# One load instead of two for the first buffer, and fifteen short reads from GpSimd, in a row-sum kernel

## The chip, the cores and the metric

The kernel runs on one core of a Trainium2 chip. The metric is device time in microseconds, the median of seven runs: 162.25 us for the kernel before (162.16 to 162.47). A core has several engines that run side by side and wait for each other through semaphores. Here VectorE (DVE) and ScalarE (ACT) add, SyncE (SP) issues the loads, and GpSimd (POOL) does next to nothing. The transfers themselves run on 16 DMA engines, which are fed by queues: one queue for the DMAs that SP issues, one for those of ScalarE.

## The reference

```python
def setup_inputs():
    batch, seq, dim = 32, 512, 1024
    return {
        "x": np.random.randn(batch, seq, dim).astype(np.float32),
    }

def reference(x: np.ndarray) -> np.ndarray:
    return np.sum(x, axis=-1).astype(np.float32)
```

The input has 16,384 rows of 1024 float32 numbers, 67.1 MB in all. The output is the sum of each row.

## The kernel before

The 16,384 rows are dealt out to 128 partitions, 128 rows each, in two blocks (`BLOCKS = (112, 16)`). In a block, each partition holds consecutive rows of x: 112 in the first block, 16 in the second. The rows are loaded into buffers `xt` of 16 rows per partition (`G = 16`, 64 KB per partition, 8 MB in all), of which there are three in turn. The first block is seven such buffers; the second is one.

For each of the first six buffers one VectorE instruction (line 43, `tensor_reduce`, in `rows_dve`) sums all 16 rows and writes 16 columns of the block's result tile `res`. Of the seventh buffer VectorE sums nine rows and ScalarE seven (line 51, one row per instruction). Then ScalarE sends the first block's result to memory (line 89).

The last buffer is loaded in five smaller pieces (lines 95 and 98: 9, 4 and 2 rows, then the last row in two parts), so that less is left to sum when the last bytes land. VectorE and ScalarE share its rows; the last ones are added in pairs of halves (line 59) with a small copy between (line 112). SP sends the last result (line 114).

What sets the order around the change:

- The first buffer is loaded in two parts. Line 78 makes the parts: row 0 of each partition, then rows 1 to 15. Both are issued at line 81, as all whole buffers are. The reduce of this buffer reads all 16 rows and waits for both parts.
- Loads of the second and third buffer need no wait. The load of the fourth waits until the first reduce is over, since it overwrites the first buffer, and so on.
- After the program is built, `tile_reduce_tiled_1024_kernel` takes the first `EARLY = 2` DMA instructions of SP out of the main part and puts them into the opening part, ahead of a barrier that all engines pass. These are the two loads of the first buffer.
- At the end SP waits for the semaphores of all DMAs, in pairs, and then all engines pass the closing barrier (line 120).

Of the kernel before, what the change touches and what calls it, by code (L numbers as in the profile page):

```python
# [1 line left out]

# [4 lines left out]

F32 = mybir.dt.float32
ADD = mybir.AluOpType.add
COPY = mybir.ActivationFunctionType.Copy  # L10
X = mybir.AxisListType.X

BLOCKS = (112, 16)
G = 16
ACT_ROWS = 7
CUT = 544
EARLY = 2


@with_exitstack  # L20
def row_sums(
    ctx: ExitStack,
    tc: tile.TileContext,
    x: bass.AP,
    out: bass.AP,
):
    nc = tc.nc
    P = nc.NUM_PARTITIONS

    x_flat = x.flatten_outer_dims()  # L30
    R, D = x_flat.shape
    C = R // P
    assert R % P == 0 and sum(BLOCKS) == C
    out_flat = out.rearrange("a (b c) -> (a b c)", c=1)

    xpool = ctx.enter_context(tc.tile_pool(name="x", bufs=3))
    rpool = ctx.enter_context(tc.tile_pool(name="res", bufs=1))
    part = rpool.tile([P, 1], F32, name="part")
    seen = rpool.tile([P, 1], F32, name="seen")
    pairs = [rpool.tile([P, D // 2], F32, name=f"pairs{i}") for i in range(3)]  # L40

    def rows_dve(xt, res, j, n, c):
        nc.vector.tensor_reduce(  # L43
            out=res[:, c : c + n],
            in_=xt[:, j * D : (j + n) * D].rearrange("p (j d) -> p j d", d=D),
            axis=X,
            op=ADD,
        )

    def sum_act(v, acc):  # L50
        nc.scalar.activation(out=v, in_=v, func=COPY, accum_out=acc)  # L51

    def rows_act(xt, res, j, n, c):
        for i in range(n):
            sum_act(xt[:, (j + i) * D : (j + i + 1) * D], res[:, c + i : c + i + 1])

    def pairs_dve(xt, a, b, first, acc, pairs):
        h = (a + b) // 2
        nc.vector.tensor_tensor_reduce(  # L59
            out=pairs[:, 0 : h - a], in0=xt[:, a:h], in1=xt[:, h:b], scale=1.0, scalar=first,  # L60
            op0=ADD, op1=ADD, accum_out=acc,
        )

    def block(r0, n):
        x_b = x_flat[r0 : r0 + P * n].rearrange("(p c) d -> p (c d)", p=P)
        out_b = out_flat[r0 : r0 + P * n].rearrange("(p c) -> p c", p=P)
        return x_b, out_b, rpool.tile([P, n], F32, name=f"res{r0}")

    full = C - G
    done = 0  # L70
    for b, n in enumerate(BLOCKS):
        x_b, out_b, res = block(done * P, n)
        final = b == len(BLOCKS) - 1
        whole = n - G if final else n
        c = 0
        while c < whole:
            m = min(G, whole - c)
            xt = xpool.tile([P, G * D], F32, tag="xt", name="xt")
            parts = (0, 1, m) if done + c == 0 else (0, m)
            for i, k in zip(parts, parts[1:]):  # L80
                nc.sync.dma_start(
                    out=xt[:, i * D : k * D], in_=x_b[:, (c + i) * D : (c + k) * D]
                )
            a = ACT_ROWS if done + c + m == full else 0
            rows_dve(xt, res, 0, m - a, c)
            rows_act(xt, res, m - a, a, c + m - a)
            c += m
        if not final:
            nc.scalar.dma_start(out=out_b, in_=res)
        done += n  # L90

    xt = xpool.tile([P, G * D], F32, tag="xt", name="xt")
    cuts = [0, 9, 13, 15]
    for i, k in zip(cuts, cuts[1:]):
        nc.sync.dma_start(out=xt[:, i * D : k * D], in_=x_b[:, (c + i) * D : (c + k) * D])  # L95
    last = 15 * D
    for i, k in ((0, CUT), (CUT, D)):
        nc.sync.dma_start(
            out=xt[:, last + i : last + k],
            in_=x_b[:, c * D + last + i : c * D + last + k],  # L100
        )

    for i, k in zip(cuts[:2], cuts[1:3]):
        h = (k - i) // 2
        rows_dve(xt, res, i, h, c + i)
        rows_act(xt, res, i + h, k - i - h, c + i + h)
    pairs_dve(xt, 13 * D, 14 * D, 0.0, res[:, c + 13 : c + 14], pairs[2])
    rows_act(xt, res, 14, 1, c + 14)
    pairs_dve(xt, last, last + CUT, 0.0, part, pairs[0])


    nc.vector.tensor_copy(out=seen, in_=part)  # L112
    pairs_dve(xt, last + CUT, last + D, part, res[:, c + 15 : c + 16], pairs[1])
    nc.sync.dma_start(out=out_b, in_=res)


def kernel(tc: tile.TileContext, x: bass.AP, out: bass.AP):
    row_sums(tc, x, out)
    tc.close()
    tc.compile()  # L120

    sp = mybir.EngineType.SP
    fn = tc.nc.m.functions[0]
    entry, body = None, None
    for blk in fn.blocks:
        ops = [i for i in blk.instructions if i.engine == sp]
        if entry is None:
            entry = blk  # L130
        elif any(i.opcode == "DMACopy" for i in ops):
            body = blk
            break
    code = list(body.instructions)
    loads = [i for i in code if i.engine == sp][:EARLY]
    for load in loads:
        assert load.opcode == "DMACopy" and not load.sync_info.on_wait
        code.remove(load)
    body.instructions = code
    code = list(entry.instructions)  # L140
    at = next(k for k, i in enumerate(code) if i.engine == sp and i.opcode == "Drain")
    code[at:at] = loads
    entry.instructions = code

# [1 line left out]
_INS = ['x']  # L146
_OUTS = [((32, 512), 'float32')]


# [23 lines left out]
```

## Time and profile before

| | |
|---|---|
| median of 7 runs | 162.25 us (162.16 to 162.47) |
| the profiled execution | 162.38 us, of which the span from first to last instruction is 160.6 us |
| VectorE busy | 121.5 us, 76% of the span |
| ScalarE busy | 17.2 us, 11% |
| GpSimd busy | 0.2 us (four small fills at the start) |
| read from memory | 67.11 MB, a mean of 418 GB/s over the span |

The profile follows one execution. It says how long each engine was busy, what ended each of its idle times, and which chain of work ended last. It also gives the DMA queues with the number and size of their packets: `q1` is the queue of SP, `q10` that of ScalarE. For each group of DMA issues it gives the time from issue to landing, which includes the time that a DMA stands behind others in its queue. "L43" is line 43 of the kernel; "x6" means six instructions.

### The profile page before, as it was taken

To read this page: it belongs to the slowest core of one execution; us is meant where nothing else is said; L and a number is where in the kernel's file an instruction comes from. 1 tells how busy PE (TensorE), PEld (TensorE's weight loads), DVE (VectorE), ACT (ScalarE), POOL (GpSimd) and SP (SyncE) were. 2 spreads that over 40 slices of the span, in tenths; PEclk is the share of its full clock that TensorE was granted. 3 is DMA by queue.
4 is the path that set the end of the run, shared out by engine and by line. 5 is a ranking of instruction groups with operands and counts; after the bars stand their busy time and mean duration, and the time that the engine had idled before them with its cause. 6 is when DMAs were issued, how large, how long until landed. Compare 5 with 4: busy or idle time off the path is not lost.

```text
span 160.6 us, 119 instructions
## 1 busy us (share of the span) xinstructions
DVE 121.5 (76%) x16; ACT 17.2 (11%) x31; POOL 0.2 (0%) x4
## 2 busy tenths in 40 slices
DVE  0000059997799958999499994999949998698874
ACT  0000000000000000000000000000000000595892
POOL 0000000000000000000000000000000000000000
DMA  9988996996996996996996996996996997998990
GB/s 375 490 367 367 490 522 261 522 522 261 522 522 261 522 506 278 522 506 278 522 506 278 522 506 278 522 506 278 522 490 294 522 473 310 441 441 367 444 384 28
DMA packets 2160, 67.18 MB, mean 418 GB/s; under 512 B 496, under 2 KB 624, under 8 KB 880
## 3 DMA queue, kind: packets, MB, share of 16 engines
q1 hardware_dynamic: 2016, 67.12, 97.1%
q10 hardware_dynamic: 144, 0.06, 0.1%
HBM read 67.11 MB, written 0.07 MB: 418 GB/s over the span
## 4 chain that ended last, share of the span: by engine, by line
DMA 75%; DVE 23%; SPq 0%; issue 0%; DVEq 0%
DMA xt<-in_x_dram 75%; DVE res L43 21%; DVE pairs L59 1%; SPq L95 0%; DVE seen L112 0%; DVE part L59 0%; DVEq L120 0%; DVE res L59 0%
## 5 line engine op out<-in xcount | busy, mean ns | idle before, releaser
L43 DVE TENSOR_REDUCE res<-xt 128x16 f32<-128x16384 f32 (+3 forms) x9 | 119.8, 13309 | 36.5 <-DMA xt<-in_x_dram 36.5
L51 ACT ACT_TABLE_LOAD x1 | 1.3, 1283 | 138.1 <-DMA xt<-in_x_dram 138.1
L51 ACT ACTIVATE xt<-xt 128x1024 f32<-128x1024 f32 x15 | 15.6, 1043 | 2.3 <-DMA xt<-in_x_dram 2.2
L51 ACT ACTIVATION_READ_ACCUMULATOR xt<-xt 128x1 f32 x15 | 2.8, 187 | 0.0
L59 DVE CUSTOM_DVE_ANT_0 pairs<-xt 128x512 f32<-128x512 f32 (+1 forms) x2 | 1.1, 567 | 0.3 <-DMA xt<-in_x_dram 0.3
L59 DVE CUSTOM_DVE_ANT_0 pairs<-xt,part 128x240 f32<-128x240 f32 x1 | 0.5, 469 | 0.0
L112 DVE COPY seen<-part 128x1 f32<-128x1 f32 x1 | 0.2, 153 | 0.0
L59 DVE DVE_READ_ACCUMULATOR2_ANT res<- 128x1 f32 x2 | 0.2, 82 | 0.0
L157 POOL MEMSET const-bfloat16-1.0<- 128x1 bf16 x1 | 0.1, 101 | 0.0
L157 POOL MEMSET const-uint8-127<- 128x1 uint8 x1 | 0.1, 101 | 0.0
L157 POOL MEMSET const-float32-0.0<- 128x1 f32 x1 | 0.1, 98 | 0.2 <-issue 0.2
L157 POOL MEMSET const-float32-1.0<- 128x1 f32 x1 | 0.1, 98 | 0.0
L59 DVE DVE_READ_ACCUMULATOR2_ANT part<- 128x1 f32 x1 | 0.1, 82 | 0.0
## 6 DMA issues: line engine op xcount, KB each, us to landing
xt<-in_x_dram SPq DMA_DIRECT2D x1, 7680.0 KB, 21.5
xt<-in_x_dram SPq DMA_DIRECT2D x1, 4608.0 KB, 32.4
xt<-in_x_dram SPq DMA_DIRECT2D x1, 2048.0 KB, 37.0
xt<-in_x_dram SPq DMA_DIRECT2D x1, 1024.0 KB, 39.0
xt<-in_x_dram SPq DMA_DIRECT2D x1, 512.0 KB, 3.8
xt<-in_x_dram SPq DMA_DIRECT2D x1, 272.0 KB, 39.2
xt<-in_x_dram SPq DMA_DIRECT2D x1, 240.0 KB, 39.3
xt<-in_x_dram SPq DMA_DIRECT2D x6, 40.8
```

Of the source, the lines that this page charges most:

```text
L43: nc.vector.tensor_reduce(out=res[:, c : c + n], in_=xt[:, j * D : (j + n) * D].rearrange("p (j d) -> p j d", d=D), axis=X, op=ADD,)
L51: nc.scalar.activation(out=v, in_=v, func=COPY, accum_out=acc)
L59: nc.vector.tensor_tensor_reduce(out=pairs[:, 0 : h - a], in0=xt[:, a:h], in1=xt[:, h:b], scale=1.0, scalar=first, op0=ADD, op1=ADD, accum ...
L112: nc.vector.tensor_copy(out=seen, in_=part)
L157: nc = _bacc.Bacc("TRN2", target_bir_lowering=False, num_devices=1)
```

## The change

The list of parts goes away, so the first buffer is loaded by one DMA of 16 rows per partition, like the others. `EARLY` becomes 1, so this one load is what stands ahead of the opening barrier.

A scratch tile `tag` is added, with 16 sections of 80 numbers in each partition (5 KB per partition). VectorE copies the first 16 columns of `res`, the result of the first buffer, into the first number of each section. Then GpSimd issues 15 DMAs that read from the start of x: the first reads 17 numbers into one partition, the second 19 numbers into each of two partitions, up to 73 numbers into each of 15 partitions. Each overwrites what the copy put into its section, so the first of them waits for the copy. Nothing reads `tag`.

In the source the new lines stand after the loop over the first block's buffers. In the built program the copy comes directly after the first reduce on VectorE, ahead of the second. GpSimd has the 15 DMAs between its opening and its closing barrier. The first waits for the copy; the ninth to fifteenth each wait for the DMA eight places before, whose semaphore they use again. At the end SP waits for eight more semaphores.

```diff
-EARLY = 2
+EARLY = 1
...
             m = min(G, whole - c)
             xt = xpool.tile([P, G * D], F32, tag="xt", name="xt")
-            parts = (0, 1, m) if done + c == 0 else (0, m)
-            for i, k in zip(parts, parts[1:]):
-                nc.sync.dma_start(
-                    out=xt[:, i * D : k * D], in_=x_b[:, (c + i) * D : (c + k) * D]
-                )
+            nc.sync.dma_start(out=xt[:, 0 : m * D], in_=x_b[:, c * D : (c + m) * D])
             a = ACT_ROWS if done + c + m == full else 0
             rows_dve(xt, res, 0, m - a, c)
             rows_act(xt, res, m - a, a, c + m - a)
             c += m
+        if done == 0:
+            lengths = (17, 19, 23, 29, 31, 37, 41, 43, 47, 53, 59, 61, 67, 71, 73)
+            tag = rpool.tile([P, 16 * 80], F32, name="tag")
+            nc.vector.tensor_copy(
+                out=tag.rearrange("p (i n) -> p i n", n=80)[:, :, 0], in_=res[:, 0:16]
+            )
+            for i, k in enumerate(lengths):
+                nc.gpsimd.dma_start(
+                    out=tag[0 : i + 1, i * 80 : i * 80 + k], in_=x_flat[0 : i + 1, 0:k]
+                )
         if not final:
             nc.scalar.dma_start(out=out_b, in_=res)
```

## The prediction

> **What bounds the kernel now.** I read the chain of waits first, with the DMA queues beside it, then the issues with their landing times, then the VectorE rows in order of time, then short stretches at both ends.
>
> ```profile
> DVE 121.5 (76%) x16; ACT 17.2 (11%) x31; POOL 0.2 (0%) x4
> q1 hardware_dynamic: 2016, 67.12, 97.1%
> q10 hardware_dynamic: 144, 0.06, 0.1%
> DMA xt<-in_x_dram 75%; DVE res L43 21%; DVE pairs L59 1%; SPq L95 0%; DVE seen L112 0%; DVE part L59 0%; DVEq L120 0%; DVE res L59 0%
> ```
>
> The chain gives VectorE 21%, but the SP queue's packets fill 97.1% of what 16 DMA engines have. That queue carries 14 DMAs (13 loads, the last store) in 2016 packets, 144 each; q10, with one store, also has 144. A DMA of 128 partitions thus leaves 128 packets and 16 more, one per DMA engine.
>
> ```profile
> xt<-in_x_dram SPq DMA_DIRECT2D x1, 7680.0 KB, 21.5
> xt<-in_x_dram SPq DMA_DIRECT2D x1, 512.0 KB, 3.8
> xt<-in_x_dram SPq DMA_DIRECT2D x6, 40.8
> out_dram<-res ACTq DMA_DIRECT2D x1, 56.0 KB, 7.4
> out_dram<-res SPq DMA_DIRECT2D x1, 8.0 KB, 1.4
> ```
>
> The six whole-buffer loads take 40.8 us from issue to landing, though VectorE gets a new buffer every 19.35 us (below): each stands a whole load in the queue, so an issue that comes some us sooner or later changes nothing.
>
> ```profile
> 22.04 17.22 DVE L43 TENSOR_REDUCE res<-xt 128x16 f32<-128x16384 f32 x1 [22.04 <-DMA xt<-in_x_dram]
> 41.32 17.22 DVE L43 TENSOR_REDUCE res<-xt 128x16 f32<-128x16384 f32 x1 [2.06 <-DMA xt<-in_x_dram]
> 60.66 17.22 DVE L43 TENSOR_REDUCE res<-xt 128x16 f32<-128x16384 f32 x1 [2.12 <-DMA xt<-in_x_dram]
> 80.01 17.22 DVE L43 TENSOR_REDUCE res<-xt 128x16 f32<-128x16384 f32 x1 [2.13 <-DMA xt<-in_x_dram]
> ```
>
> Every reduce waits 2.06 to 2.14 us for a landing. From 60.66 to 80.01 is 19.35 us for 8192 KB.
>
> ```profile
> 0.43 0.42 SPq L81 DMA_DIRECT2D xt<-in_x_dram  x1
> ...
> 0.00:1.00 1.00, 0.00 (x0) 0.00 (x0) 0.20 (x4) 1.00 0.00 0
> 1.00:2.00 1.00, 0.00 (x0) 0.00 (x0) 0.00 (x0) 1.00 0.91 164
> ...
> 40.30:59.65 19.35, 17.22 (x1) 0.00 (x0) 0.00 (x0) 1.00 1.00 434
> 158.80:160.00 1.20, 0.00 (x0) 0.00 (x0) 0.00 (x0) 1.00 0.08 7
> ```
>
> The first line, from the timeline, is SP's second issue, at 0.43. The others are stretches: start and end, length, busy us of three engines, clock, DMA share, GB/s. In a middle stretch of one load's length the DMA share is 1.00 at 434 GB/s. So the end is set by one line: the start of the stream, plus 65,536 KB and everything else the DMA engines must carry, plus the tail. A change is worth what it adds to or takes from the DMA engines' time, at the ends or in between; work on VectorE counts for nothing until it exceeds 2.06 us in a period.
>
> **The change part by part.** The sum is made against the profiled execution's 162.38 us (span 160.6, about 1.8 around it). That is 0.13 over the median of 162.25, to which I carry the difference over.
>
> *One load for the first buffer.* A 512 KB and a 7680 KB load become one of 8192 KB. Line 43's first reduce needs all 16 rows, so it waited for both parts already: no earlier start is lost. At the stream's rate (19.35 us / 8192 KB) 7680 KB take 18.14 us. Measured: issued at 0.43 and landed 21.5 later, at about 21.94, against 3.8 for the first part: 18.14, full rate. The 512 KB would take 1.21 at that rate and landed at 3.8; 2.59 us of that is starting up. What changes in the middle is only one packet per engine less, 0.02 us at the prices below. What is open is the start-up. An 8 KB store needs 1.4 us in all, so 2.59 - 1.4 = 1.19 us were lost because the first pieces ran at half speed (2.4 us instead of 1.21; the stretch 1.00:2.00 shows 164 GB/s). If a long first piece hides all of that, the change gains 1.19. If the half speed lasts for the first piece whatever its length, it now lasts for 19.35 / 8 = 2.42 us of data instead of 1.21, and costs 1.2 more. Ends -1.2 and +1.2, nothing in the trace nearer to one: I take the middle, and with the packet -0.02.
>
> SP also issues one DMA less before the barrier; the loads of buffers two and three go out about 0.4 us sooner and are not due before 21.9. With the cover of a whole load gone, it would be worth that 0.4.
>
> *The copy on VectorE* (new line 87) stands right after the first reduce. The nearest row is the 128x1 copy at line 112, 153 ns; 16 elements add, by 2286 ns for 2048 (1.1 ns each), 0.02: 0.17 us. It lies in the 2.06 us before the second reduce. Behind it on VectorE stands only that reduce; the SP load of the fourth buffer waits for the first reduce, not for the copy. Without that idle time it would cost 0.17. Only GpSimd's first read waits for it.
>
> *Fifteen issues on GpSimd* begin at about 39.5 (22.04 + 17.22 + 0.17). GpSimd has nothing else until the closing barrier. The trace has no GpSimd issue; the nearest are ACT's store and SP's loads. From both sides: 15 x 0.37 us if an issue is like ACT's (372 ns on its queue, from the store's rows), so done at 45; or 15 x 7.4 = 111 us if each waited for a landing like that of ACT's store in the loaded stream, so done at 151. Both are before 158.7, when SP's closing waits begin, and nothing reads the scratch tile: no cost on the path. I take a date near 60 to 95, as from the ninth on each read waits for the landing of the eighth before it.
>
> *What the reads put on the DMA engines.* 1 + 2 + ... + 15 = 120 pieces, and 15 x 16 = 240 closing packets if these DMAs close on 16 engines as all those in the trace do; 22.5 packets per engine, 7.5 with data. Prices: the last store's 144 packets take a share of 0.08 in 1.2 us on 16 engines: 0.08 x 1.2 x 16 / 144 = 11 ns each (64 B and closing packets). q10's 144 take 0.1% (0.05 to 0.15) of 160.6 x 16: 18 ns, 9 to 27 (448 B). The new pieces have 68 to 292 B, between the two. Low: 15 closing packets x 11 = 0.165, 7.5 x 11 = 0.08: 0.25. High: 0.165 + 7.5 x 27 = 0.37. I take 18 for the data: 0.30 us. As the engines have no free time in these stretches, it is paid in full and every later landing moves with it. That q10's store cost the loads no more than its packets' own time is seen in its stretch, where the DMA share stays at 1.
>
> *The end.* SP's closing waits go through eight more semaphores in pairs. Most pass while the store is under way; one more pair stands behind the store's own. A wait there takes 28 ns and SP's gaps between instructions in the chain are 0.05: 0 to 0.08 us, taken as 0.06.
>
> **A rule against it, and one on the issues.** The row comes first: the 56 KB store sat in a full queue, and the share of q10 was 0.1% of the engines' time, 0.24 us per engine at most (0.15% of 160.6). The Trainium skill, DMA: Bandwidth & Descriptors, sections "Anatomy of one DMA" and "Rules for kernel authors", gives each DMA a fixed cost of about 2.0 us and says that under 64 KB one pays mostly overhead; were that time of the engines, an estimate from the page would be 15 x 2.0 = 30 us and a total near 192. The page puts most of it into waiting for the write receipt, which the store's row bears out, so the sum stays. The other row is VectorE's 17.22 of every 19.35 us. SBUF — State Buffer, section "SBUF: two separate sides", says that some VectorE operations keep GpSimd from writing descriptors. No run here shows whether this reduce does; by the rule the issues would wait for the 2.1 us gaps and the sum would not change.
>
> Sum: -0.02 + 0.30 + 0.06 = +0.34 us, 162.72 for an execution like the profiled one, 162.59 against the median: +0.21%.
>
> **The rivals.**
>
> *The reads are cheaper.* If GpSimd's DMAs close only on the engines that carry their data, there are 240 packets, 15 per engine at 11 ns: 0.165, and with the closing pair hidden 162.25 + 0.165 - 0.02 = 162.40, no change that can be told. For it: the trace shows only DMAs that use all engines. Against: all 15 DMAs there close on 16.
>
> *Faster: the single load hides the start-up.* Place: the first 4 us, price up to 1.19, so 162.59 - 1.19 = 161.40; halfway, 162.0. It decides from a gain of 0.66 on (162.59 to 161.93). For it: 164 GB/s in the second us, in short pieces. Against: the engines were starting from nothing, which a long piece meets too.
>
> *Slower by more: the half speed lasts longer*, or short reads from HBM hold an engine longer than the short stores that gave the prices. The first costs up to 1.2: 163.8; halfway, 163.2. Against the second: q10's row.
>
> *The change misses its place*: reads so late that they meet the tail. The later date above, 151, is still under a full queue, so the price is the same 0.30; no time of its own.
>
> **How the numbers follow.** A measurement here can tell about 0.2% from no change, so 161.93 to 162.57 is "same". Forecast (162.6, just above that edge): 0.38. Cheaper reads: 0.36. Faster: 0.14. Slower by more: 0.12. Slower in all is 0.38 + 0.12 = 0.50, same 0.36, faster 0.14. The range goes from 161.9, where half of the start-up's gain is in, to 163.3, where half of its loss is: that leaves out no more than 2 in 10, most of it at full gain or full loss.
>
> **What would show it.** First landing: the first reduce still at 22.04 (within 0.1) if the split is worth nothing; near 20.9 or 23.2 if a start-up rival holds. The reads: a third queue with 360 packets (240 in the rival); the reduces' starts 19.35 apart at first, then a period or several that are longer by 0.30 together between 40 and 95. The end: the time from the last pairs to the span's end longer by 0.06. VectorE's second reduce still idles for about 1.9. It would be wrong if the periods grew by more than 0.4 in all, or the first landing moved by over 0.3.

## The result and the profile after

The changed kernel takes 162.80 us (median of 13 runs, 162.58 to 163.75) against 162.25 for the kernel before on the same chip (32 runs, 162.10 to 162.63). The ratio is 1.0040, with a 95% interval of 1.0031 to 1.0049: slower by 0.5 to 0.8 us. The forecast was 162.6, slower. The runs of the changed kernel also lie further apart: 1.2 us from lowest to highest, against 0.5 before.

The profiled execution took 162.69 us (span 160.9). From its page, two of the DMA queues (packets, MB, share of the 16 engines' time) and GpSimd's issues (count, busy us and mean ns of one, idle us before):

```profile
q1 hardware_dynamic: 1872, 67.12, 97.1%
q0 software_dynamic: 480, 0.03, 0.2%
...
L91 POOL DMA_DIRECT2D tag<-in_x_dram x15 | 7.8, 526 | 67.6 <-DVE tag L87 39.1
```

SP's queue has 144 packets less, one DMA. GpSimd's queue `q0` is new, with 480 packets: 32 for each of the 15 DMAs, not the 16 plus its data that the prediction counted. Its share rounds to 0.2% of 160.9 us, 0.24 to 0.40 us per engine; in the packet records that the trace keeps it is 0.33. The copy on VectorE took 182 ns.

VectorE and GpSimd in order of time (start, busy us, engine, line; in brackets the idle time before and what ended it):

```profile
21.84 17.22 DVE L43 TENSOR_REDUCE res<-xt 128x16 f32<-128x16384 f32 x1 [21.84 <-DMA xt<-in_x_dram]
39.10 0.18 DVE L87 COPY tag<-res 128x16 f32<-128x16 f32 x1
39.59 4.20 POOL L91 DMA_DIRECT2D tag<-in_x_dram  x8 [39.15 <-DVE tag L87]
41.16 17.22 DVE L43 TENSOR_REDUCE res<-xt 128x16 f32<-128x16384 f32 x1 [1.88 <-DMA xt<-in_x_dram]
48.70 0.52 POOL L91 DMA_DIRECT2D tag<-in_x_dram  x1 [4.91 <-DMA tag<-in_x_dram]
53.54 0.52 POOL L91 DMA_DIRECT2D tag<-in_x_dram  x1 [4.33 <-DMA tag<-in_x_dram]
...
60.57 17.22 DVE L43 TENSOR_REDUCE res<-xt 128x16 f32<-128x16384 f32 x1 [2.19 <-DMA xt<-in_x_dram]
...
80.14 17.22 DVE L43 TENSOR_REDUCE res<-xt 128x16 f32<-128x16384 f32 x1 [2.35 <-DMA xt<-in_x_dram]
99.50 17.22 DVE L43 TENSOR_REDUCE res<-xt 128x16 f32<-128x16384 f32 x1 [2.14 <-DMA xt<-in_x_dram]
```

The copy and the issues lie in VectorE's idle time and beside its reduces, as predicted. The landings tell the rest. From 41.16 to 60.57 is 19.41 us, to 80.14 another 19.57, to 99.50 19.36; before, all these were about 19.35. From the second reduce (41.16) to the reduce of the seventh buffer (138.22) it is 97.06 us, against 96.75 before (41.32 to 138.07): 0.31 us that the DMA engines spent on something else, close to the 0.33 of queue `q0`. GpSimd's waits show how the short reads travel: the ninth and tenth issue are 4.84 us apart, two turns of 2.42 us, each behind one 64 KB packet (an inference from the times; between the eleventh and the twelfth it is 2.61, about one turn). The issues themselves are not held back by VectorE's reduces, which the prediction left open: six of the last seven lie inside a reduce and take 0.52 us like the one that does not. The last issue is at 75.4, and it lands 33.8 us later, at 109: far from the tail.

The close, in the rows of line 126 (count, shortest / median / longest ns, first and last start):

```profile
L126 SPq EVENT_SEMAPHORE  x11: 17/28/28, 158.9 to 160.8; - x11
...
L126 POOLq DRAIN  x3: 40/107/34512, 75.3 to 160.6; - x3
...
L126 POOLq EVENT_SEMAPHORE_RANGE_CLEAR  x1: 136/136/136, 160.5 to 160.5; - x1
```

In the kernel before, SP had 7 such waits, GpSimd's longest drain took 70 ns and its clearing of semaphores 93 ns. Now it is 11 waits, and GpSimd too takes somewhat longer: a drain of 107 ns (34.5 us is the drain that waits beside the loads) and 136 ns for the clearing. From the issue of the last store to the end of the span it is 2.45 us, against 2.29 before.

So far the profiled executions differ by 0.31 us: 0.20 earlier at the first landing (22.04 to 21.84), 0.04 later from there to the second reduce, 0.31 later in the periods and 0.16 later behind the last store's issue. But the medians differ by 0.55. Whether the first landing really came earlier, and where the scatter comes from, only runs of the parts can tell.

### The profile page after: what moved, and what is told of

It is laid out like the page before. It is cut to its first block, busy times and chain, and to the rows that moved or that the text cites. A ratio compares the mean times of both kernels' runs of the same rounds, so it can differ in the third digit from the quotient of the medians.

```text
span 160.9 us, 137 instructions
## 1 busy us (share of the span) xinstructions
DVE 121.7 (76%) x17; ACT 17.2 (11%) x31; POOL 8.0 (5%) x19
## 4 chain that ended last, share of the span: by engine, by line
DMA 75%; DVE 22%; SPq 0%; issue 0%; DVEq 0%
DMA xt<-in_x_dram 75%; DVE res L43 21%; DVE pairs L59 1%; SPq L101 0%; DVE seen L118 0%; DVE part L59 0%; DVEq L126 0%; DVE res L59 0%
## 5 line engine op out<-in xcount | busy, mean ns | idle before, releaser
L91 POOL DMA_DIRECT2D tag<-in_x_dram x15 | 7.8, 526 | 67.6 <-DVE tag L87 39.1
```

The source lines that it names most:

```text
L91: nc.gpsimd.dma_start(out=tag[0 : i + 1, i * 80 : i * 80 + k], in_=x_flat[0 : i + 1, 0:k])
```

## Experiments

Every run was timed in turn with the kernel before on its chip; the ratio is to that.

| run | median, lowest to highest (runs) | before | ratio, 95% interval |
|---|---|---|---|
| two loads, reads | 162.81, 162.59 to 164.60 (12) | 162.13 | 1.0056, 1.0034 to 1.0077 |
| one load | 162.38, 162.29 to 162.49 (11) | 162.13 | 1.0012, 1.0003 to 1.0020 |
| one load, copy | 162.38, 162.22 to 162.63 (11) | 162.13 | 1.0016, 1.0007 to 1.0024 |
| both (the changed kernel) | 162.73, 162.64 to 162.91 (5) | 162.13 | 1.0034, 1.0022 to 1.0046 |
| one partition each | 162.60, 162.47 to 163.21 (12) | 162.16 | 1.0025, 1.0016 to 1.0034 |
| fifteen partitions each | 163.41, 163.31 to 163.74 (5) | 162.16 | 1.0074, 1.0061 to 1.0088 |
| last read only | 162.51, 162.31 to 162.70 (11) | 162.16 | 1.0020, 1.0011 to 1.0028 |
| rows 1024 apart | 163.81, 163.57 to 163.93 (4) | 162.16 | 1.0098, 1.0083 to 1.0114 |
| fifteen partitions, all 17 numbers | 163.42, 163.31 to 163.62 (5) | 162.19 | 1.0075, 1.0062 to 1.0087 |
| fifteen partitions, all 73 numbers | 164.89, 163.75 to 166.08 (6) | 162.19 | 1.0165, 1.0127 to 1.0204 |
| half a row first | 162.24, 162.09 to 163.03 (12) | 162.19 | 1.0007, 0.9996 to 1.0018 |
| rows 1025 apart | 162.83, 162.75 to 163.08 (5) | 162.14 | 1.0044, 1.0031 to 1.0058 |

### The parts of the change

*Two loads, with the copy and the reads* (the kernel before, plus the new block):

```diff
+        if done == 0:
+            lengths = (17, 19, 23, 29, 31, 37, 41, 43, 47, 53, 59, 61, 67, 71, 73)
...
         if not final:
```

> The first buffer keeps its two loads; the copy and the fifteen reads are added. Theory (the reads and the longer close are a fixed sum): +0.3 for the packets and about +0.13 at the end, nothing taken off at the start: 162.7 us, with the runs within 0.5 us of each other, as those of before are. Rival, the single load makes the runs scatter: also 162.7 and narrow. Rival, the reads make the runs scatter (after's 13 runs reach from 162.58 to 163.75): a spread of over 1 us here, median 162.8 or more.

*One load* (the changed kernel without the copy and the reads):

```diff
-        if done == 0:
-            lengths = (17, 19, 23, 29, 31, 37, 41, 43, 47, 53, 59, 61, 67, 71, 73)
...
         if not final:
```

> One load for the first buffer, no copy and no reads. Theory: the first reduce starts at 21.84 as in after, 0.2 sooner than before, and all later landings move with it: 162.1 us, narrow. Rival, the single load makes the runs scatter: median 162.2 to 162.5, some runs a full us above the lowest. Rival, the reads make them scatter: 162.1, narrow.

*One load and the copy*:

```diff
-            for i, k in enumerate(lengths):
-                nc.gpsimd.dma_start(
-                    out=tag[0 : i + 1, i * 80 : i * 80 + k], in_=x_flat[0 : i + 1, 0:k]
-                )
```

> One load and the copy into the scratch tile, no reads (nothing is read into the scratch tile). Theory: the copy lies in VectorE's idle time before the second reduce, so the same as the one load alone, within 0.1 us. If the copy is on the path it shows as +0.2 over that.

*Both*, the changed kernel again:

> The changed kernel itself, on the same chip as its parts. Theory: the sum of the parts, 162.25 - 0.1 + 0.45 = 162.6 to 162.8. If the scatter belongs to this combination alone, only this one reaches 163.1 and more.

One load alone is not faster, as the theory had it, but slower, by 0.25 us in the medians (0.05 to 0.32 by the interval). The profile of the kernel before had misled: it is one execution, of 162.38 us, above the median, and its first reduce started late, at 22.04. In the run with two loads and reads, which has the same two loads, it starts at 21.65, and with half a row first, below, at 21.73. The eleven profiled executions with one load have it between 21.81 and 22.10. VectorE in order of time, two loads with the reads:

```profile
21.65 17.22 DVE L43 TENSOR_REDUCE res<-xt 128x16 f32<-128x16384 f32 x1 [21.65 <-DMA xt<-in_x_dram]
40.92 17.22 DVE L43 TENSOR_REDUCE res<-xt 128x16 f32<-128x16384 f32 x1 [1.84 <-DMA xt<-in_x_dram]
```

and one load alone:

```profile
21.92 17.22 DVE L43 TENSOR_REDUCE res<-xt 128x16 f32<-128x16384 f32 x1 [21.92 <-DMA xt<-in_x_dram]
41.25 17.22 DVE L43 TENSOR_REDUCE res<-xt 128x16 f32<-128x16384 f32 x1 [2.11 <-DMA xt<-in_x_dram]
```

0.27 us between these two first landings. That is one pair of executions, and single ones differ by as much among themselves, so the pair does not prove where the 0.25 of the medians arises. Short stretches of one load alone show the slow start (start and end, length, busy us of three engines, clock, DMA share, GB/s; packets count where they start):

```profile
1.00:2.00 1.00, 0.00 (x0) 0.00 (x0) 0.00 (x0) 1.00 3.15 1049
...
4.00:5.00 1.00, 0.00 (x0) 0.00 (x0) 0.00 (x0) 1.00 2.42 1049
```

1049 GB/s in 1 us is 16 packets of 64 KB, one per DMA engine. The first 16 hold their engines for 3.15 us on average, the next 16 for 2.42: the slow start costs 0.73 us per engine (0.62 to 0.74 in the eleven executions with one load). Counted the same way in the packet records, as time above 2.42 us per 64 KB, it costs 0.44 in the run with two loads and reads, 0.56 with half a row first and 0.62 in the kernel before: less with small first pieces, by some 0.1 to 0.2, an estimate from three executions.

Two smaller parts of the 0.25 hardly scatter. From the first to the second reduce it is 19.31 to 19.35 us in every profile with one load and 19.27 to 19.28 in the three with two; why is open. And the close is longer: from the issue of the last store to the end of the span it is 2.29 us in both kernels with two loads and no reads, 2.37 in both with one load and no reads. SP's waits from 159.6 us on, in the kernel before, with one load alone, and with two loads and the reads (count, shortest / median / longest ns, first and last start):

```profile
L120 SPq EVENT_SEMAPHORE  x4: 17/22/28, 159.7 to 160.5; - x4
...
L116 SPq EVENT_SEMAPHORE  x5: 17/28/28, 159.7 to 160.6; - x5
...
L130 SPq EVENT_SEMAPHORE  x4: 17/22/28, 160.0 to 160.9; - x4
```

Two of these waits belong to the closing barrier. The others begin once the last store has landed: two with two loads, three with one, each about 0.06 us after the one before. SP waits for the semaphores in pairs, and with one DMA fewer the store's stands in an earlier pair.

The copy costs nothing that shows: 162.38 with it and without. Both together are 0.35 above that (162.73), which is the price of reads and close behind one load.

In the other order the parts come out differently. With two loads the same copy and reads cost 0.68 (162.81 against 162.13), and with the reads in place the single load costs nothing that shows (162.73 against 162.81, with intervals that overlap). The lowest runs say the same: 161.99 before, 162.29 with one load, 162.59 with two loads and reads, 162.64 with both. So 0.25 and 0.35 are the parts in one order only, and why the reads cost more behind two loads is open.

The scatter came with the reads: without them none of the 22 runs here is above 162.63, with them and two loads three of twelve are at 163.65 and more. So it doesn't need the single load. (One run of twelve without any reads, half a row first, below, stands at 163.03; the reads are not the only thing that can do it.)

### What of the reads costs time

*One partition each*:

```diff
-                    out=tag[0 : i + 1, i * 80 : i * 80 + k], in_=x_flat[0 : i + 1, 0:k]
+                    out=tag[0:1, i * 80 : i * 80 + k], in_=x_flat[0:1, 0:k]
```

> One load, copy, fifteen reads, but each into one partition only (15 pieces of data instead of 120; the scratch tile gets less). Before was 162.13 and one load with the copy 162.38 in the runs so far. Theory (every GpSimd DMA leaves 32 packets, and these are what is paid): 465 four-byte packets at 9 ns and 15 pieces at 17 are 0.28 us per DMA engine, and 0.1 more at the close: 162.75, as with the changed kernel. Rival (the pieces of data do it, by slowing the 64 KB packets that run beside them): few long 64 KB packets, 162.5 to 162.6, and the runs within 0.4 us of each other.

*Fifteen partitions each*:

```diff
-                    out=tag[0 : i + 1, i * 80 : i * 80 + k], in_=x_flat[0 : i + 1, 0:k]
+                    out=tag[0:15, i * 80 : i * 80 + k], in_=x_flat[0:15, 0:k]
```

> One load, copy, fifteen reads, each into fifteen partitions (225 pieces of data instead of 120). Theory (packets alone): 225 pieces at 17 ns and 255 at 9 are 0.38 us per engine, 162.85. Rival (pieces slow the long packets): twice the extra, 163.0 to 163.3, wide scatter. If the number of pieces of one read is what matters, 64 KB packets of over 2.5 us stand beside the first reads too; if their length does (over some 200 B), only beside the last six, as in the changed kernel.

*The last read only*:

```diff
-            for i, k in enumerate(lengths):
+            for i, k in list(enumerate(lengths))[14:]:
```

> One load, copy, and only the last of the fifteen reads (73 numbers into 15 partitions). Theory: 2 packets per engine, 0.03 us, and about 0.1 at the close, 162.5, narrow. If use of GpSimd's queue by itself brings the scatter, single runs of 163 and more appear here too.

*Rows 1024 apart*:

```diff
-                    out=tag[0 : i + 1, i * 80 : i * 80 + k], in_=x_flat[0 : i + 1, 0:k]
+                    out=tag[0 : i + 1, i * 80 : i * 80 + k], in_=x_flat[0 : 1024 * i + 1 : 1024, 0:k]
```

> The changed kernel, but the short reads take their numbers from rows 1024 apart (4 MB) instead of the first rows of x, which lie 4 KB apart. Theory (packets): 162.75 and the same scatter as the changed kernel. Rival (the pieces of one read meet each other in one place of memory): the long 64 KB packets beside the last reads go away, 162.6 and narrow.

With one piece of data per read the queue still has 480 packets:

```profile
q0 software_dynamic: 480, 0.00, 0.2%
```

Every GpSimd DMA leaves 32 here, one of them with data and 31 of 4 bytes. That would be two for each of 16 engines; the trace does not name the engines. Over one load with the copy the cost is 0.22 us (162.60 against 162.38, two chips whose kernels before differ by 0.03). The packets' sum had been 0.28 and the close 0.1: too much, though of the right size. The rival's 162.5 to 162.6 fits better, but not its narrow runs: one of the twelve took 163.21. With 15 pieces per read instead of one it is 1.03 (163.41), where the packets would have given 0.48. So the pieces cost more than their own time once many go out together: the packet theory fell for this kernel, and the rival held, with more than the 163.0 to 163.3 it had named and without the wide scatter (0.43 us among five runs). One read alone costs 0.13 in the medians (162.51), on two chips and with intervals that overlap. Its profile shows 0.03 us of packets per engine and 0.08 at the close (2.45 us from the store's issue against 2.37), where GpSimd's drain and clearing take 98 and 136 ns instead of 70 and 93. Its runs do not scatter, so the use of GpSimd's queue alone brings neither the 1.03 nor the scatter.

Rows 1024 apart went against both theories. They had said 162.75 or 162.6, and it was 163.81: the reads cost more, not less, when their pieces lie 4 MB apart.

### Length or time

*Fifteen partitions, all reads of 17 numbers*, against the run with fifteen partitions:

```diff
-            lengths = (17, 19, 23, 29, 31, 37, 41, 43, 47, 53, 59, 61, 67, 71, 73)
+            lengths = (17,) * 15
```

> One load, copy, fifteen reads of 17 numbers (68 B) into fifteen partitions each. Theory (it is the length of the pieces, over some 150 to 200 B, that makes the 64 KB packets beside them long): no 64 KB packet of over 2.5 us beside any read, and packets alone, 0.31 us per engine: 162.75. Rival (it is a matter of when: only reads after about 72 us do it): long packets from 72 to 108 as with fifteen partitions and growing lengths, 163.2 to 163.4.

*All reads of 73 numbers*:

```diff
-            lengths = (17, 19, 23, 29, 31, 37, 41, 43, 47, 53, 59, 61, 67, 71, 73)
+            lengths = (73,) * 15
```

> One load, copy, fifteen reads of 73 numbers (292 B) into fifteen partitions each. Theory (length): long 64 KB packets beside the first reads too, from 45 us on, and more in all than with growing lengths (163.41): 163.6 to 164. Rival (when): none before 72 us, 163.4. Packets alone would be 0.42 us per engine, 162.9.

Neither theory is right as it stood. Reads of 68 B cost as much as growing ones (163.42 and 163.41), so a length over 150 B is not needed; reads of 292 B cost 1.5 us more (164.89), so length counts (its six runs lie between 163.75 and 166.08, and the profiled one took 165.65). VectorE in order of time, all 17 numbers:

```profile
60.74 17.22 DVE L43 TENSOR_REDUCE res<-xt 128x16 f32<-128x16384 f32 x1 [2.25 <-DMA xt<-in_x_dram]
80.28 17.22 DVE L43 TENSOR_REDUCE res<-xt 128x16 f32<-128x16384 f32 x1 [2.32 <-DMA xt<-in_x_dram]
99.74 17.22 DVE L43 TENSOR_REDUCE res<-xt 128x16 f32<-128x16384 f32 x1 [2.23 <-DMA xt<-in_x_dram]
119.50 17.22 DVE L43 TENSOR_REDUCE res<-xt 128x16 f32<-128x16384 f32 x1 [2.55 <-DMA xt<-in_x_dram]
```

and all 73:

```profile
41.19 17.22 DVE L43 TENSOR_REDUCE res<-xt 128x16 f32<-128x16384 f32 x1 [1.89 <-DMA xt<-in_x_dram]
61.11 17.22 DVE L43 TENSOR_REDUCE res<-xt 128x16 f32<-128x16384 f32 x1 [2.70 <-DMA xt<-in_x_dram]
81.91 17.22 DVE L43 TENSOR_REDUCE res<-xt 128x16 f32<-128x16384 f32 x1 [3.58 <-DMA xt<-in_x_dram]
```

With equal short reads the periods are 19.54, 19.46 and 19.76: the last is the worst, though it meets only the last reads. A buffer counts as landed when its last piece is there, so the periods do not date the long packets: in the records those over 2.5 us start between 69 and 106 us. With long reads the periods are 19.92 and 20.80 from the start. In the second, the stretch that begins 64 KB packets beside a read, and the next one, where the engines carry only the load and closing packets (same columns as above):

```profile
62.30:63.30 1.00, 1.00 (x1) 0.00 (x0) 0.00 (x0) 1.00 2.83 1053
```

```profile
64.90:65.90 1.00, 1.00 (x1) 0.00 (x0) 0.00 (x0) 1.00 2.47 1049
```

16 packets of 64 KB with 15 pieces of 292 B (1053 GB/s in 1 us) hold the engines for 2.83 us, without the pieces 2.47. The pieces' own time is 0.02 us each: the 64 KB packets that start with them are what gets long, and all 16 of them do (2.77 to 2.83 us by the records). Summed over the profiled execution, the 64 KB packets after the first 16 take 0.10 to 0.11 us per engine above 2.418 us each with one load and no reads, 0.52 with fifteen partitions, 0.51 with 17 numbers, 0.73 with rows 1024 apart and 3.03 with 73 numbers. That is where the time goes in these kernels. The changed kernel beside its fourteenth read, in the execution of the result and in that of the run "both":

```profile
100.70:101.70 1.00, 1.00 (x1) 0.00 (x0) 0.00 (x0) 1.00 2.45 1053
...
100.70:101.70 1.00, 1.00 (x1) 0.00 (x0) 0.00 (x0) 1.00 2.50 1053
```

2.45 and 2.50: little of the kind; over the whole execution it sums to 0.17 and 0.31 us per engine. In the run with two loads and the reads, some 64 KB packets beside the last seven reads are long, by up to 0.27 us each. Why the first reads of a run do no harm (beside the first two no packet is long even with 73 numbers) stays open, and so does what makes single runs of these kernels a full us longer: no profile was taken of such a run of the changed kernel.

### The distance between the rows, and a smaller first piece

*Rows 1025 apart*, against the run with 1024:

```diff
-                    out=tag[0 : i + 1, i * 80 : i * 80 + k], in_=x_flat[0 : 1024 * i + 1 : 1024, 0:k]
+                    out=tag[0 : i + 1, i * 80 : i * 80 + k], in_=x_flat[0 : 1025 * i + 1 : 1025, 0:k]
```

> As the run with rows 1024 apart (163.81), but 1025 apart: 4 MB and 4 KB, so that the pieces of a read no longer lie at a distance that is a power of two. Theory (the exact 4 MB made its pieces wait for each other): 162.7 to 162.9, as the changed kernel with rows next to each other. Rival (being far apart is enough): 163.6 to 164.

162.83, against 163.81: with 4 KB added to the distance of 4 MB, the loss is gone and the time is that of the changed kernel. The theory's number held. That the pieces wait for each other is not shown: their own packets take 16 and 17 ns on average in the two runs, and it is again the 64 KB packets that differ, by 0.73 against 0.24 us per engine. The Trainium skill has this for large copies: DMA: Bandwidth & Descriptors, section "Latency and other measured facts", tells of rates halved at a row pitch of 4 MiB and restored by 4 KiB more, with the cause inferred. These two runs agree with it, for pieces of only 68 to 292 B, at 1.0 us.

*Half a row first*, in the kernel before:

```diff
-            parts = (0, 1, m) if done + c == 0 else (0, m)
+            parts = (0, D // 2, m * D) if done + c == 0 else (0, m * D)
             for i, k in zip(parts, parts[1:]):
-                nc.sync.dma_start(
-                    out=xt[:, i * D : k * D], in_=x_b[:, (c + i) * D : (c + k) * D]
-                )
+                nc.sync.dma_start(out=xt[:, i:k], in_=x_b[:, c * D + i : c * D + k])
```

> The kernel before, with its first load cut to half a row (256 KB instead of 512) and the second longer by as much; no copy, no reads. If what the split saves is that the stream's slow start falls on small pieces, a smaller first piece saves as much or a little more: 162.0 to 162.2. If two DMAs alone (whatever their size) are what helps, 162.16 as before. If the small piece is too short to cover the slow start, part of the single load's loss comes back: 162.25 to 162.4.

162.24 against 162.19, an interval that includes no change: two loads with a first piece of half the size do as well, or nearly. Whether the size of the first piece matters or only that there are two DMAs, this run cannot tell: no run has two loads with large pieces. It doesn't beat the kernel before, and no run here points to a version that does.

## Why the prediction was right, and where it was off

- *What sets the end.* Right: the DMA engines, at their limit from start to end. What was added to them in the middle came out in the landings, and VectorE's copy (182 ns, 0.17 predicted) did not.
- *One load for the first buffer.* This is the mis-sized term: taken as -0.02 us, "the middle" between -1.2 and +1.2, measured +0.25 by itself (0.05 to 0.32); with the reads in place none of it shows. The start-up was read off one execution with a late first landing, so the split looked worth nothing. The half of the argument that held is that the slow start falls on the first pieces whatever their length: 0.62 to 0.74 us per engine with long ones, not the 1.2 more of "half speed". Two parts were not in the sum: 0.05 up to the second reduce and 0.08 at the close. And "one packet per engine less" does not fit the prediction's own count: 144 packets less are nine for each of 16 engines. A saving from them shows in no run.
- *The reads.* 0.30 for the packets, where their records have 0.33 and the periods of the profiled execution grew by 0.31 (by 0.46 in the run "both"). The count was wrong (480 packets, not 360), the prices were a little high (9 ns for 11, 17 for 18), and the two errors met by luck. The prices leave out what many pieces do to the packets beside them; in the two profiled executions of the changed kernel that is about 0.06 and 0.2 us per engine more than without reads. In the medians reads and close cost 0.35 behind one load and 0.68 behind two, so a sum of fixed parts is itself only a rough account.
- *The close.* 0.06 predicted, for the eight more semaphores; 0.16 in the profiles (2.45 against 2.29). Those semaphores pass while the store is under way. The pair of waits that did come on top belongs to the single load (0.08), and GpSimd's longer drain and clearing (0.08) were not in the sum.
- *GpSimd's issues.* 0.52 us each, between the two bounds, done at 76 and hidden.
- *The fixed cost of about 2 us per DMA* that the Trainium skill states (DMA: Bandwidth & Descriptors, section "Anatomy of one DMA") is not the engines' time: 15 DMAs cost 0.35 us with one load, 0.68 with two, not 30.
- *The signs.* The second reduce idles 1.88 us (1.9 named) and the periods grew by 0.31 (0.30 named). The first landing moved by 0.20, more than the 0.1 that stood for a split worth nothing, though in one execution that says little. The 480 packets fit neither count. The ends of the range, 161.9 and 163.3, lie 0.1 outside the halves that the rivals' own sums give (162.0 and 163.2).
- *The rivals.* The cheaper reads (240 packets) are out: even one piece leaves 32 packets. The faster rival is out: the single load gains in no run. Of the slower one, the slow start is there, at less than its price. Short reads that hold an engine longer are not: their own packets take what was priced, and it is the 64 KB packets beside them that get long, most of all with 15 pieces in every read.

162.59 was forecast; the parts as measured in one order give 162.25 + 0.25 + 0.35 = 162.85, against 162.80. The direction came from the reads, as argued. The forecast was low by 0.21, and the single load's term alone accounts for 0.27 in this order.

## What to carry to other kernels

Where the DMA engines are the bound from the first to the last microsecond, a tiny DMA isn't free: each of GpSimd's cost 32 packets and together they made the close longer, and where many pieces go out at once they slow the large packets beside them. Cutting the first load in two was worth 0.25 us here without the reads, even though nobody waits for the first piece alone; part of that is where the last store stands among the closing waits, so the number of DMAs matters there and not only their size. And a start-up of 1 us must not be read off one execution, nor a part's price off one order of the parts: run each part by itself and together with the others, on the chip of the kernel it is compared with.

## What was not expected of the hardware

- A GpSimd DMA leaves 32 packets whether it fills one partition or fifteen (480 for 15 DMAs of one partition each); one from SP or ScalarE with 128 partitions leaves 144.
- The first 16 packets of 64 KB take 3.15 us on average with one load alone, the next 16 take 2.42.
- Fifteen pieces of 292 B make the 16 packets of 64 KB that start with them 0.36 us longer (2.83 against 2.47), although the pieces themselves take 0.02.
- Short reads from rows 4 MB apart cost 1.0 us more in all than from rows 4 MB and 4 KB apart.
- One DMA fewer lengthened the close by 0.08 us (2.29 to 2.37 from the last store's issue).
